# Four query blocks as two Strassen pairs ahead of the last gate pair

## The chip, the cores and the metric

The kernel runs on one core of a Trainium2 chip. The metric is device time in microseconds (us) of one execution. TensorE does the matrix products, VectorE (DVE in the profile) and ScalarE (ACT) the elementwise work, GpSimd (POOL) a few copies, and SyncE (SP) issues most of the DMA. Each engine has its own queue of instructions and works through it in order; an instruction waits at the head of its queue until the semaphores of what it needs have come. The order on each queue is fixed when the kernel is built: the code is written in some order, and a scheduler then arranges the instructions of each engine.

## The reference, cut to what matters

The layer mixes a prompt of 1024 tokens and 8 sample tokens (1032 columns, `TT`) by three branches that share one input projection, and merges them with gates.

```python
def mixer_block(xn, mem_k, mem_v, ...):
    sc_b, sc_c, sc_x, z, xbc, dt_raw, q, gates = jnp.split(xn @ w_in, splits, axis=-1)
    conv_u, sc_new = causal_depthwise_conv(sc_c * sc_x, sc_hist, sc_conv_w)
    y_a = (sc_b * conv_u) @ w_sc_out
    ...
    y_ssd, ssm_new = ssd_fn(xs, dt, a, bm, cm, ssm_s0)
    y_ssd = (y_ssd + ssm_d[:, None] * xs).reshape(bsz, seq, SSM_D_INNER) * jax.nn.silu(z)
    y_b = group_rmsnorm(y_ssd, ssm_norm_w, SSM_GROUPS) @ w_ssm_out
    qh = q.reshape(bsz, seq, ATTN_HEADS, ATTN_HEAD_DIM)
    scores = jnp.einsum('blhd,bmhd->bhlm', qh, mem_k).astype(jnp.float32) * (ATTN_HEAD_DIM ** -0.5)
    probs = jax.nn.softmax(scores, axis=-1).astype(mem_v.dtype)
    y_c = jnp.einsum('bhlm,bmhd->blhd', probs, mem_v).reshape(bsz, seq, ATTN_DIM) @ w_attn_o
    g_a, g_b, g_c = jnp.split(jax.nn.sigmoid(gates), N_BRANCHES, axis=-1)
    merged = g_a * y_a + g_b * y_b + g_c * y_c
    return merged @ w_merge_o, (sc_new, ssm_conv_new, ssm_new)
```

All is float32. `q` is 1024 columns of the projection, computed as eight blocks of 128 columns, 0 to 7. The change concerns how blocks 0 to 3 are computed, and what runs beside the scan (`ssd_fn`) after that.

## The kernel before, in words

**Products.** A float32 product is done as three products of a rounded high part and a low remainder (`hi*hi`, `hi*lo`, `lo*hi`). ScalarE casts the high part, VectorE subtracts it to get the low one, for weights (`weights`, lines 175 and 176) as for activations (`split_act`, lines 185 and 186). Activations lie transposed: 128 channels on partitions, 1032 tokens along the free side, 8 such tiles for 1024 channels.

There are two ways to do a block of 128 output columns:
- A *plain block* (`gemm3`, matmul in line 254): 8 input tiles, the columns in three thirds of 344, three products, so 72 matmuls of 128x344. `q_step`, `out_part` and others use it.
- A *Strassen pair* (`strassen`, with `st_prod`, matmul in line 306): two neighbouring blocks at once by 7 products of half size. Each product is 4 input tiles by three products by two halves of a 516-column half row (256 and 260 columns), so 168 matmuls for two blocks. The sums of the input halves (`xforms`) are made once for all pairs; the sums of the weight halves are made per pair by VectorE and ScalarE. `plain_pair` wraps it for the blocks of z and of the gates, applies the activation function and writes the two blocks to DRAM.

**The part of the program that matters here**, by the profiled execution:
- Projections in Strassen pairs, up to `gate_pair(22)`. Its hook `plain` fetches the weights of the first plain block, calls `load_group(0)` and remakes one set of the sums.
- The *scan stage*. 18 plain blocks run on TensorE: the eight query blocks wq0 to wq7, then the conv branch's output wo00 to wo07 (inputs: the eight tiles of `sc_d`), then wo10 and wo11 of the first half of the scan branch's output (inputs: tiles 0 to 7 of `yb_d`). In between, the pieces in the list `pend` are issued: for each of four groups (0 to 3) the scan's steps over eight chunks (`ssd_pieces`: small matmuls, then y and s updates, lines 1091 to 1149), the final state (`psf`, line 1165), four `z_pieces` (multiply by the silu of z and sum the squares into `sqa`, lines 1221 to 1232) and the group's norm (`group_norm`: three matmuls `psny`, line 1244, that average `sqa` over channels; then scaling, line 1267, and the stores to `yb_d`, line 1270).
- The *attention stage*: blocks wo12 to wo17, and wo20 to wo27 (second half of the scan branch, inputs: tiles 8 to 15 of `yb_d`), with the attention's pieces in between. Among them is the sample tokens' attention (`pso`, line 1726: one matmul group per sample over a freshly loaded megabyte of cached values, and `psob`, line 1743, which transposes the sample rows for the store to `at_d`).
- wo30 onwards: the attention branch's output, inputs `at_d`, and the rest of the layer.

**What sets the order.** `tick` issues the next piece of `pend`. A block that starts takes `pace[0]` pieces (with the fraction carried on in `pace[1]`) and spreads them evenly over its 24 steps (`marks`). Before the scan stage `pace` is set to the number of pieces divided by a number of blocks, so this number decides where in the sequence of blocks each piece falls. For the attention stage line 1845 sets it to the number of its pieces divided by the number of blocks left before wo30, less 1.4. When the first block of a new set of inputs starts (wo00, wo10, wo20, wo30), `out_in` loads and splits what `out_ahead` has not yet: `out_ahead`, called in the last block of the set before, loads two tiles and splits as the last third of that block goes along. A piece that is issued in the same stretch shares VectorE, ScalarE and SyncE's queue with these loads and splits. Weights of the next block are loaded one block ahead (`run_next`).

Of the kernel before, what the change touches and what calls it, by code (L numbers as in the profile page):

```python
# [11 lines left out]
AF = mybir.ActivationFunctionType  # L12
# [5 lines left out]
P = 128  # L18
D = 1024
T = 1024  # L20
NS = 8
TT = T + NS
# [4 lines left out]
KD = D // P  # L27
EPS = 1e-6
LAG = 3

QS = -1.0 / 16.0
GROUPS = 4
HEADS = 32
HPG = 8
# [5 lines left out]
C_SCB, C_SCC, C_SCX, C_Z, C_XBC, C_DT, C_Q, C_G = 0, 1024, 2048, 3072, 5120, 8192, 8224, 9248  # L40
# [3 lines left out]
def tile_kernel(ctx: ExitStack, tc, a, o):  # L44
    nc = tc.nc
    V, S, G, PE, SY = nc.vector, nc.scalar, nc.gpsimd, nc.tensor, nc.sync
# [95 lines left out]
    loaded = {}  # L142

    def load_raw(src, name):
        raw = wp.tile([P, 1024], F32, tag="raw", name=name + "r")
        if len(src.shape) == 3:
            in_turn("raw", SY.dma_start(raw.rearrange("p (k c) -> p k c", k=src.shape[1]), src))
        else:
            in_turn("raw", SY.dma_start(raw, src))
        return raw  # L150
# [28 lines left out]
    def ev_tile(name, shape=(P, TT + 4), dt=F32):  # L179
        return ev.tile(list(shape), dt, tag="ev", name=name)  # L180
# [8 lines left out]
    pend = deque()  # L189
# [12 lines left out]
    pace = [3, 0.0]  # L202
# [55 lines left out]
    def wblock(w, col):  # L258
        return w[:, col : col + P].rearrange("(k p) c -> p k c", p=P)
# [5 lines left out]
    HS = [slice(0, HT), slice(HT, TT)]  # L265
# [211 lines left out]
    q_d = dram("q_d", [8, P, TT])  # L477
# [10 lines left out]
    qs = cp.tile([P, 8, NS], F32, tag="qs", name="qs")  # L488

    w_in = a["w_in"][0]  # L490
# [456 lines left out]
        S.activation(t[:, :TT], flat(ps), AF.Silu)  # L947
        S.dma_start(zs_d[i], t[:, :TT])

    def plain_pair(col, dst, i, nm, func, hook=None, after_t3=None):  # L950

        os = []

        def outs():
            os.extend([pa_["u"](f"{nm}{i}"), pa_["u"](f"{nm}{i + 1}")])
            return os[0][:, HS[0]], os[0][:, HS[1]], None, os[1][:, HS[1]]

        pa = strassen(
            wblock(w_in, col + i * P), wblock(w_in, col + (i + 1) * P), xforms, f"{nm}{i}", pa_["s"], outs,
            hook=hook, after_t3=after_t3,  # L960
        )
        S.activation(os[0][:, :TT], os[0][:, :TT], func)
        S.dma_start(dst[i], os[0][:, :TT])
        S.activation(os[1][:, HS[1]], os[1][:, HS[1]], func)
        ins = S.activation(os[1][:, HS[0]], pa, func, scale=-1.0).ins
        S.dma_start(dst[i + 1], os[1][:, :TT])
        return ins

    def z_pair(i, hook=None):
        plain_pair(C_Z, zs_d, i, "Z", AF.Silu, hook)  # L970

    def gate_pair(i, after_t3=None):
        return plain_pair(C_G, gt_d, i, "G", AF.Sigmoid, None, after_t3)
# [495 lines left out]
    with_steps(3, lambda: gate_pair(18))  # L1469
    with_steps(2, lambda: gate_pair(20))  # L1470
    assert not steps
    rb = ev_tile("rb")
    SY.dma_start(rb[:, :TT], r_d.to_broadcast([P, TT]))
    b12s = []
# [14 lines left out]
            xg.append(t)  # L1489

    def plain():
        loaded["wq0"] = load_raw(wblock(w_in, C_Q), "wq0")
        load_group(0)
        for kt in range(4):
            split_to(*xforms["T3"][kt], b12s[kt // 2][:, HS[kt % 2]])
# [9 lines left out]
    for name in ("ssr", "ssd", "ssy"):  # L1505
        pool[name] = ssd.enter_context(tc.tile_pool(name=name, bufs=2, side="right"))
    fillers = deque()
    for i in range(8):
        fillers.extend(q_step(i))

    acts = []
# [67 lines left out]
    ins = ((sc_d, a["w_sc_out"][0]), (yb_d, a["w_ssm_out"][0, 0:D]), (yb_d[8:16], a["w_ssm_out"][0, D : 2 * D]), (at_d, None))  # L1579
# [15 lines left out]
    for g in range(GROUPS):  # L1595
# [8 lines left out]
        if g == GROUPS - 1:  # L1604
            norm[2] = lambda f=norm[2]: (f and f(), kv_ahead(0))
        pend.extend(z_pieces(g, xg, hold) + [None] + norm)
    pace[:] = len(pend) / (len(fillers) + KD + 2) + 1e-6, 0.0
    while fillers or pend:
        if len(fillers) == 1:
            out_ahead(sc_d)  # L1610
# [414 lines left out]
    for m in (0, 2):  # L2025
        nm = f"wm{m}"
        raw1, raw2, sa, wA, wS = begun if m == 0 else st_begin(wm[m], wm[m + 1], nm, ev_sums)
        residuals(m)
        pa, pb = (whole(mm_ps(nm + n)) for n in "ab")
# [34 lines left out]
    for m in last:  # L2064
        nm = f"wm{m}"
# [119 lines left out]
    for n, (j, j2) in enumerate(pairs):  # L2185
        s1, s2, pa = hidden_pair("g", j, j2)
# [3 lines left out]
        u1, u2, pa = hidden_pair("u", j, j2)  # L2190
# [34 lines left out]
    after_t3 = [None]  # L2225
# [258 lines left out]
```

## Time and profile before

| | |
|---|---|
| time, median of 3 runs | 2417.18 us (2413.96 to 2420.94) |
| the profiled execution's own time | 2418.97 us |
| its span (first to last instruction) | 2417.2 us |
| TensorE busy, 0 to 940 us | 930.14 |
| TensorE busy, 940 to 980 us (G20, G22) | 39.97 |
| TensorE busy, 980 to 1313 us (scan stage) | 329.58 of 333 |
| TensorE busy, 1313 to 1549 us (attention stage) | 230.61 of 236 |
| TensorE busy, 1549 to 2417 us (wo30 and the rest) | 858.04 of 868.2 |
| bytes moved, mean over the span | 167 GB/s |

The span is what the profiler saw between the first and the last instruction; 1.8 us of the profiled execution lie outside it. "PE" in a row is TensorE, "PEld" its weight loads. A row of the chain of waits has the start, the time on the chain, the engine, what ran (output, and input behind an arrow) and the line. A row of a timeline has the start, the duration, the engine, the line, the operation, the tiles and their shapes, and in square brackets the engine's idle time ahead of it and what ended it. A row of a table of windows has the stretch, its length, then for TensorE, its weight loads, VectorE, ScalarE and GpSimd the busy time and the number of instructions, then the granted TensorE clock, the share of DMA time and GB/s.

### The profile page before, as it was taken

The page shows a single profiled execution, that of the slowest core. Times are in us where ns is not written, and L with a number is a line of the kernel's source. Part 1 is how long each engine was busy: PE and PEld are TensorE (multiplying, and loading weights), DVE is VectorE, ACT ScalarE, POOL GpSimd, SP SyncE. Part 2 cuts the span into 40 slices and gives each one's busy share as a digit, 9 for nine tenths or more (in the row PEclk, how much of TensorE's full clock was granted, in tenths as well). Part 3 has the DMA queues.
Part 4 walks back from the last instruction along what each step waited for, and adds up shares of the span by engine and source line. Part 5 has one row for each costly group of instructions (what it writes and reads, how often), then busy time and mean ns, then how long its engine had stood idle before and what let it go on. Part 6 is the DMA issues. An engine that isn't in the chain of part 4 may idle for free.

```text
span 2417.2 us, 45099 instructions
## 1 busy us (share of the span) xinstructions
PE 2388.3 (99%) x18620; PEld 2305.3 (95%) x18620; DVE 1650.5 (68%) x2700; ACT 1101.1 (46%) x1794; POOL 129.3 (5%) x163
## 2 busy tenths in 40 slices
PE   8999999999999999999999999999999999999998
PEld 6999999999999999998998998899999999999998
DVE  6844677777777676568788664469687655567965
ACT  6643454555453543656656443214553333343423
POOL 0000000000000000223212000000000000000000
PEclk9999999999999999999999999999999999999999
DMA  6445423444354345768787787864346333354622
GB/s 201 140 149 166 132 88 115 134 147 128 109 158 119 101 140 167 234 214 279 257 286 238 234 321 242 276 215 145 118 159 175 103 96 105 93 182 151 194 90 78
DMA packets 348244, 403.74 MB, mean 167 GB/s; under 512 B 16014, under 2 KB 269054, under 8 KB 348031
## 3 DMA queue, kind: packets, MB, share of 16 engines
q1 hardware_dynamic: 324902, 337.60, 45.1%
q10 hardware_dynamic: 23137, 63.26, 6.8%
q8 instruction: 146, 2.39, 0.4%
q14 instruction: 59, 0.48, 0.1%
HBM read 284.65 MB, written 116.38 MB: 166 GB/s over the span
## 4 chain that ended last, share of the span: by engine, by line
PE 89%; DMA 4%; DVE 4%; ACT 1%; issue 1%; SPq 0%; ACTq 0%; DVEq 0%
PE po L254 8%; PE po L226 3%; PE ps_q L254 3%; PE pd L2295 1%; PE py L1130 1%; PE po L1121 1%; PE ps_z L226 1%; PE pss L1143 1%; PE G16m L306 1%; PE d00m L306 1%; PE G22m L306 1%; PE Z2m L306 1%; PE Z14m L306 1%; PE X4m L306 1%; PE Z12m L306 1%
## 5 line engine op out<-in xcount | busy, mean ns | idle before, releaser
L1073 ACT ACTIVATE r<-r,acum 128x128 f32<-128x128 f32 x256 | 79.3, 392 | 3.0 <-DMA r<-ac_d 2.4
L1106 POOL TENSOR_TENSOR xdd<-xdt,decst 128x512 f32<-128x512 f32 x32 | 51.1, 1596 | 248.3 <-DVE xdt L1102 246.1
L860 DVE SCALAR_TENSOR_TENSOR ax<-u,prm,ax 128x1024 f32<-128x1024 f32 x44 | 56.3, 1280 | 0.0
L1014 ACT ACTIVATE st<-st,es 128x128 f32<-128x128 f32 x128 | 41.4, 392 | 21.9 <-DMA st<-in_state_ssm_dram 19.1
L1564 DVE TENSOR_TENSOR yr<-po,yr 128x344 f32<-128x344 f32 x24 | 12.1, 514 | 45.9 <-PE po L254 32.5
L1100 DVE TENSOR_TENSOR r<-r,cbm 128x1024 f32<-128x1024 f32 x32 | 39.0, 1218 | 3.2 <-ACT r L1075 2.4
L1016 DVE SCALAR_TENSOR_TENSOR st<-sr,dts,st 128x128 f32<-128x128 f32 x128 | 40.3, 346 | 0.4
L1125 DVE TENSOR_TENSOR y<-po,ea 128x512 f32<-128x512 f32 x28 | 19.3, 689 | 25.4 <-PE po L1121 25.3
L1020 DVE SCALAR_TENSOR_TENSOR sr<-st,sr 128x128 f32<-128x128 f32 x128 | 35.3, 286 | 1.1
L1130 PE MATMUL py<-r,xdt 128*64 128x128 f32 x512 | 35.0, 279 | 0.7 <-DVE xdt L1102 0.7
L1676 DVE SCALAR_TENSOR_TENSOR kc<-kc,qb 128x256 f32<-128x256 f32 x64 | 24.2, 420 | 16.6 <-DMA qb<-qs_d 11.0
L1156 POOL TENSOR_TENSOR s<-s,cdec 128x512 f32<-128x512 f32 x28 | 34.8, 1244 | 4.1 <-DVE s L1149 3.5
L1143 PE MATMUL pss<-xdd,bT 128*128 128x512 f32 x64 | 33.0, 597 | 1.1 <-DVE y L1125 0.6
L1075 ACT ACTIVATE r<-r 128x1024 f32<-128x1024 f32 x32 | 33.8, 1056 | 0.6
L1130 PEld LDWEIGHTS py<-r,xdt 128*64 128x64 f32 x512 | 27.3, 136 | 5.0 <-DVE xdt L1102 1.4
L1121 PE MATMUL po<-bc,s 128*128 128x128 f32 x224 | 30.2, 278 | 0.8 <-DVE s L1149 0.8
L1121 PEld LDWEIGHTS po<-bc,s 128*128 128x128 f32 x224 | 28.0, 191 | 2.4 <-DVE s L1149 1.7
L1688 ACT ACTIVATE pr<-psa,mx 128x256 f32<-128x256 f32 x32 | 14.9, 473 | 29.7 <-DVE mx L1686 29.7
L863 DVE SCALAR_TENSOR_TENSOR ax<-u,prm,ax 128x1032 f32<-128x1032 f32 x22 | 28.3, 1287 | 0.0
L857 ACT ACTIVATE ax<-u,prm 128x1024 f32<-128x1024 f32 x22 | 27.4, 1246 | 1.2 <-ACT u L941 0.4
L1791 ACT CAST pTh<-psp 128x256 fp32r<-128x256 f32 x32 | 11.8, 374 | 32.9 <-DVE pTl L1792 24.0
L1102 DVE TENSOR_TENSOR xdt<-xp,dtT 128x512 f32<-128x512 f32 x32 | 22.0, 687 | 6.4 <-PE xp L1095 5.8
(8856 smaller groups left out, 9294.4 us busy)
## 6 DMA issues: line engine op xcount, KB each, us to landing
r<-ac_d SPq DMA_DIRECT2D x32, 512.0 KB
gt_d<-G ACTq DMA_DIRECT2D x24, 516.0 KB
gt<-gt_d SPq DMA_DIRECT2D x24, 516.0 KB
xs_d<-ax ACTq DMA_DIRECT2D x22, 516.0 KB
zs<-zs_d SPq DMA_DIRECT2D x16, 516.0 KB
yb_d<-x SPq DMA_DIRECT2D x16, 516.0 KB
in<-yb_d SPq DMA_DIRECT2D x16, 516.0 KB
st<-in_state_ssm_dram SPq DMA_DIRECT2D x32, 256.0 KB
```

The lines of the kernel that those rows point to most:

```text
L226: PE.matmul(po, wt[:, ks], xc, start=(k == 0 and i == 0), stop=(k == nk - 1 and i == 2))
L254: PE.matmul(pss[t][:, :CW], wt[:, ks], x[:, c], start=(k == 0 and i == 0), stop=(k == nk - 1 and i == 2))
L306: last_mm[0] = PE.matmul(po, wt[:, ks], xc, start=(start and kt == 0 and i == 0), stop=(kt == 3 and i == 2), skip_group_check=True,).ins
L860: V.scalar_tensor_tensor(acc[:, :T], u[:, j : j + T], w[j], acc[:, :T], op0=ALU.mult, op1=ALU.add)
L1014: S.activation(st[:, i], st[:, i], AF.Copy, scale=es[:, g * 4 + i, b : b + 1])
L1016: V.scalar_tensor_tensor(st[:, i], rb, dts[:, g * 4 + i, b : b + 1], st[:, i], op0=ALU.mult, op1=ALU.add)
L1073: S.activation(r[:, j, :], r[:, j, :], AF.Relu, scale=-1.0, bias=acum[:, c, h : h + 1])
L1100: V.tensor_tensor(r, r, bc(cbm.unsqueeze(1), [P, HPG, P]), op=ALU.mult)
L1106: G.tensor_tensor(b3(xdd, HPG), b3(xdt, HPG), bc(decst[:, c, hs].unsqueeze(2), [P, HPG, 64]), op=ALU.mult)
L1121: last = PE.matmul(po[:, t * P : (t + 1) * P], state["s"][:, t * P : (t + 1) * P], bcg[1][:, cs], start=True, stop=True,)
L1130: PE.matmul(py[hp : hp + 64, (h // 2) * P : (h // 2 + 1) * P], xdt[:, h * 64 : (h + 1) * 64], r[:, (h % 2) * 4 + h // 2, :], start=True, s ...
L1143: PE.matmul(pss, bT, xdd, start=True, stop=True)
```

## The change

Query blocks 0 to 3 are computed as two Strassen pairs, Q0 and Q2, between `gate_pair(20)` and `gate_pair(22)`. `plain_pair` gets a scale for them, and GpSimd copies the eight sample columns of each block to `qs`, which `q_step` does for a plain block. The plain blocks of the scan stage begin with wq4. The number that sets the pace is that of the fillers (now 4) plus 12 in place of plus 10: the scan's pieces are spread over 16 blocks, wq4 to wq7, wo00 to wo07 and wo10 to wo13, in place of 18. The attention stage gets 12 blocks, wo14 to wo27, in place of 14.

```diff
+QP = 4
...
-    def plain_pair(col, dst, i, nm, func, hook=None, after_t3=None):
+    def plain_pair(col, dst, i, nm, func, hook=None, after_t3=None, scale=1.0):
...
-        S.activation(os[0][:, :TT], os[0][:, :TT], func)
+        S.activation(os[0][:, :TT], os[0][:, :TT], func, scale=scale)
+        if dst is q_d:
+            G.tensor_copy(qs[:, i, :], os[0][:, T:TT])
         S.dma_start(dst[i], os[0][:, :TT])
-        S.activation(os[1][:, HS[1]], os[1][:, HS[1]], func)
-        ins = S.activation(os[1][:, HS[0]], pa, func, scale=-1.0).ins
+        S.activation(os[1][:, HS[1]], os[1][:, HS[1]], func, scale=scale)
+        if dst is q_d:
+            G.tensor_copy(qs[:, i + 1, :], os[1][:, T:TT])
+        ins = S.activation(os[1][:, HS[0]], pa, func, scale=-scale).ins
...
+    def q_pair(i):
+        plain_pair(C_Q, q_d, i, "Q", AF.Copy, scale=QS)
...
     with_steps(2, lambda: gate_pair(20))
     assert not steps
+    for i in range(0, QP, 2):
+        q_pair(i)
...
-        loaded["wq0"] = load_raw(wblock(w_in, C_Q), "wq0")
+        loaded[f"wq{QP}"] = load_raw(wblock(w_in, C_Q + QP * P), f"wq{QP}")
...
-    for i in range(8):
+    for i in range(QP, 8):
         fillers.extend(q_step(i))
...
-    pace[:] = len(pend) / (len(fillers) + KD + 2) + 1e-6, 0.0
+    pace[:] = len(pend) / (len(fillers) + KD + 4) + 1e-6, 0.0
```

**How the order moves.** In the rows below, a name ends in the scheduler's own number; po07 is the output of block wo07, b03 is the split input tile 3 of the running set (h high, l low), in03 its load. Lines of the kernel after stand 1 to 10 lower down than before.

The first place is the change of inputs from wo07 to wo10. In VectorE's queue of the kernel before, the subtractions of wo10's inputs stand among the scan steps of group 3 (y3, s3, r3, cbm3) and the gate products of wo07:

```order
L186 TENSOR_TENSOR b03l_14410<-in03_14345,b03h_14409 128x1032
L186 TENSOR_TENSOR b04l_14439<-in04_14376,b04h_14438 128x1032
L1125 TENSOR_TENSOR y3_14022<-po3_3_14265,ea3_3_14213 128x4x128
L1097 TENSOR_TENSOR cbm3_4_14307<-bp3_4_14299,tri_79 128x128
L1135 TENSOR_TENSOR y3_14022<-py3_3_14271,y3_14022 128x4x128
L1100 TENSOR_TENSOR r3_4_14141<-r3_4_14141,cbm3_4_14307 128x1024
L1102 TENSOR_TENSOR xdt3_4_14312<-xp3_4_14302,dtT_768 128x512
L1149 TENSOR_TENSOR s3_3_14244<-pss3_3_14324,s3_3_14244 128x512
L1560 TENSOR_TENSOR gt07_14200<-po07_0_14210,gt07_14200 128x344
L1560 TENSOR_TENSOR gt07_14200<-po07_1_14211,gt07_14200 128x344
L186 TENSOR_TENSOR b05l_14472<-in05_14413,b05h_14471 128x1032
```

In the kernel after, the same subtractions stand among the last pieces of group 2, x20 to x23 with the squares sqa2, behind the last chunk's y2 and s2:

```order
L1229 SCALAR_TENSOR_TENSOR x20_13383<-x20_13383,dpar_773,y2_13481 128x1032
L1157 TENSOR_TENSOR s2_7_14000<-pss2_7_14062,s2_7_14000 128x512
L1232 TENSOR_TENSOR x20_13383<-x20_13383,zs20_14011 128x1032
L1229 SCALAR_TENSOR_TENSOR x21_13386<-x21_13386,dpar_773,y2_13481 128x1032
L1229 SCALAR_TENSOR_TENSOR x22_13389<-x22_13389,dpar_773,y2_13481 128x1032
L1232 TENSOR_TENSOR x21_13386<-x21_13386,zs21_14013 128x1032
L1232 TENSOR_TENSOR x22_13389<-x22_13389,zs22_14091 128x1032
L1229 SCALAR_TENSOR_TENSOR x23_13392<-x23_13392,dpar_773,y2_13481 128x1032
L1240 TENSOR_TENSOR sqa2_14089<-sqa2_14089,zs21_14013 128x1032
L1232 TENSOR_TENSOR x23_13392<-x23_13392,zs23_14106 128x1032
L1240 TENSOR_TENSOR sqa2_14089<-sqa2_14089,zs22_14091 128x1032
L187 TENSOR_TENSOR b02l_14150<-in02_14115,b02h_14149 128x1032
```

On TensorE the means of that group (psny20 to psny22) now stand behind the tenth matmul of wo10:

```order
L255 MATMUL po10_0_14235<-b01h_14130,wo10l_14232 128x344
L255 MATMUL po10_0_14235<-b02h_14149,wo10h_14231 128x344
L255 MATMUL po10_0_14235<-b02l_14150,wo10h_14231 128x344
L255 MATMUL po10_0_14235<-b02h_14149,wo10l_14232 128x344
L255 MATMUL po10_0_14235<-b03h_14170,wo10h_14231 128x344
L1252 MATMUL psny20_14161<-sqa2_14089,ones_77 128x344
L1252 MATMUL psny21_14164<-sqa2_14089,ones_77 128x344
L1252 MATMUL psny22_14182<-sqa2_14089,ones_77 128x344
```

What moved is the end of group 2: it now falls in the block in which the inputs change. Before, the means of groups 0 to 3 stood in wq4 (behind 44 of its 72 matmuls), wo01 (27), wo05 (42) and wo11 (72); now they stand in wo00 (17), wo04 (46), wo10 (10) and wo14 (46).

The second place is the change of inputs from wq7 to wo00, where group 0 now ends. VectorE's queue of the kernel after has the subtractions b02l to b06l between the pieces of x02, x03 and sqa0 (line 1253 behind them reads the mean psny00):

```order
L1232 TENSOR_TENSOR x02_11586<-x02_11586,zs02_12396 128x1032
L187 TENSOR_TENSOR b02l_12442<-in02_12405,b02h_12441 128x1032
L1229 SCALAR_TENSOR_TENSOR x03_11588<-x03_11588,dpar_773,y0_11783 128x1032
L1240 TENSOR_TENSOR sqa0_12394<-sqa0_12394,zs02_12396 128x1032
L1232 TENSOR_TENSOR x03_11588<-x03_11588,zs03_12414 128x1032
L187 TENSOR_TENSOR b03l_12461<-in03_12426,b03h_12460 128x1032
L187 TENSOR_TENSOR b04l_12485<-in04_12445,b04h_12484 128x1032
L1240 TENSOR_TENSOR sqa0_12394<-sqa0_12394,zs03_12414 128x1032
L187 TENSOR_TENSOR b05l_12510<-in05_12464,b05h_12509 128x1032
L187 TENSOR_TENSOR b06l_12524<-in06_12488,b06h_12523 128x1032
L1253 TENSOR_SCALAR y0_11783<-psny00_12475 128x344
```

Before, group 0 ended in wq4, where no inputs are split, and these subtractions stood among the steps of the last two chunks of group 1 (py1_6 and py1_7), whose norm followed in wo01.

The third place is the end of the sample tokens' attention, ahead of wo30. On TensorE the transposes psob stand behind 4 of wo27's 72 matmuls in the kernel before:

```order
L254 MATMUL po27_0_17093<-b00h_15780,wo27h_17089 128x344
L254 MATMUL po27_0_17093<-b00l_15781,wo27h_17089 128x344
L254 MATMUL po27_0_17093<-b00h_15780,wo27l_17090 128x344
L254 MATMUL po27_1_17094<-b00h_15780,wo27h_17089 128x344
L1743 MATMUL psob_17025<-ident_72,osr_17023 128x8 x8
L254 MATMUL po27_1_17094<-b00l_15781,wo27h_17089 128x344
L254 MATMUL po27_1_17094<-b00h_15780,wo27l_17090 128x344
```

and behind 29 of them in the kernel after:

```order
L255 MATMUL po27_2_17171<-b02h_15791,wo27h_17165 128x344
L255 MATMUL po27_2_17171<-b02l_15792,wo27h_17165 128x344
L255 MATMUL po27_2_17171<-b02h_15791,wo27l_17166 128x344
L255 MATMUL po27_0_17169<-b03h_15819,wo27h_17165 128x344
L255 MATMUL po27_0_17169<-b03l_15820,wo27h_17165 128x344
L1753 MATMUL psob_17101<-ident_72,osr_17099 128x8 x8
L255 MATMUL po27_0_17169<-b03h_15819,wo27l_17166 128x344
L255 MATMUL po27_1_17170<-b03h_15819,wo27h_17165 128x344
```

So 68 matmuls of wo27 stood between psob and the first matmul of wo30, and now 43 do.

## The prediction

> **What bounds the kernel now.** I read the page's span, busy shares and chain first.
>
> ```profile
> span 2417.2 us, 45099 instructions
> PE 2388.3 (99%) x18620; PEld 2305.3 (95%) x18620; DVE 1650.5 (68%) x2700; ACT 1101.1 (46%) x1794; POOL 129.3 (5%) x163
> PE 89%; DMA 4%; DVE 4%; ACT 1%; issue 1%; SPq 0%; ACTq 0%; DVEq 0%
> ```
>
> TensorE is busy in 2388.3 of 2417.2 us: time goes down if it gets less work, and up if it pauses. So I looked next at how the two stages that change are filled, and how close the others come to holding TensorE up (table of windows: stretch, length, then TensorE, weight loads, VectorE, ScalarE, GpSimd, clock, DMA share, GB/s).
>
> ```profile
> 940.00:960.00 20.00, 20.00 (x170) 20.00 (x170) 11.23 (x15) 7.80 (x11) 0.00 (x0) 1.00 0.35 111
> 980.00:1313.00 333.00, 329.58 (x2357) 299.07 (x2356) 256.07 (x318) 198.74 (x417) 94.71 (x68) 1.00 0.77 250
> 1130.00:1160.00 30.00, 29.49 (x191) 27.89 (x191) 28.45 (x32) 17.26 (x24) 1.90 (x2) 1.00 0.91 311
> 1313.00:1549.00 236.00, 230.61 (x1539) 215.78 (x1538) 125.64 (x306) 90.21 (x192) 0.00 (x0) 0.99 0.78 263
> ```
>
> Over the scan stage TensorE idles 3.4 us in 333. But in 1130 to 1160, where group 1 of the scan ends, VectorE is busy 28.45 of 30 us: there it is as full as TensorE, and anything added to it in such a stretch must show.
>
> **What is removed.** Four plain blocks become two Strassen pairs. The chain of waits (start, us on the chain, engine, tile, line, count) gives both pitches.
>
> ```profile
> 940.10 20.02 PE G20m L306 x168
> 1051.17 12.14 PE ps_q L254 x77
> ```
>
> A pair is 168 matmuls in 20.02 us; a plain matmul takes 12.14/77 = 157.7 ns, so a block of 72 takes 11.35 us and four take 45.4. Two pairs take 40.04. **Saving: 5.4 us.** The work that comes with a pair (weight sums, splits, scaling) lies under its matmuls: beside G20 VectorE had 11.23 and ScalarE 7.80 of 20 us to do, DMA .35. I cost it at nothing, and the GpSimd copies of 8 columns too, since GpSimd is idle there. Without that cover a pair would cost at most VectorE's 11.23 us, which no row suggests.
>
> **What moves.** The same scan pieces stand over 16 blocks. VectorE's timeline shows what the end of a group asks of it (group 1, before).
>
> ```profile
> 1133.70 0.68 DVE L1135 TENSOR_TENSOR y<-py,y 128x512 f32<-128x512 f32 x1
> 1134.30 1.22 DVE L186 TENSOR_TENSOR b06l<-in,b06h 128x1032 fp32r<-128x1032 f32 x1
> 1135.44 0.68 DVE L1149 TENSOR_TENSOR s<-pss,s 128x512 f32<-128x512 f32 x1
> 1136.04 2.48 DVE L1221 SCALAR_TENSOR_TENSOR x<-x,dpar,y 128x1032 f32<-128x1032 f32 x2
> 1138.44 2.37 DVE L1224 TENSOR_TENSOR x<-x,zs 128x1032 f32<-128x1032 f32 x2
> 1140.73 1.22 DVE L186 TENSOR_TENSOR b07l<-in,b07h 128x1032 fp32r<-128x1032 f32 x1
> ...
> 1148.88 1.35 DVE L1560 TENSOR_TENSOR gt<-po,gt 128x344 f32<-128x344 f32 x3
> 1150.15 1.23 DVE L1232 TENSOR_TENSOR sqa<-sqa,zs 128x1032 f32<-128x1032 f32 x1
> ```
>
> ```profile
> 1136.17 0.66 PE L1165 MATMUL psf<-ident,s 128*128 128x128 f32 x4 [0.51 <-DVE s L1149]
> 1151.64 1.90 PE L1244 MATMUL psny<-sqa,ones 128*128 128x344 f32 x6
> ```
>
> From the last y at 1133.70 to the end of the last sum of squares at 1151.38 VectorE runs back to back for 17.68 us, and TensorE's means (psny) start 0.26 us behind it. By the starts of neighbouring rows a pitch is 0.6 us for y and s, 1.2 for a piece's first multiply, 1.15 for its second, for a sum and for a subtraction of inputs, and 1.27 for the three gate products.
>
> *wo00.* Group 0 now ends where the inputs change. Without b06l, b07l and the gate products of that row, but with five subtractions (b00l to b04l) in front of psny00, the chain is 17.68 - 1.14 - 1.15 - 1.27 + 5 x 1.15 = 19.9 us. TensorE has in front of psny00 the last 72 matmuls of wq7 and 17 of wo00: 89 x 0.1577 = 14.0 us, with psf 0.66 and the state product:
>
> ```profile
> 1254.81 1.12 PE pss L1143 x2
> ```
>
> 1.1 us, together 15.8. **Pause: 4.1 us**, in one place or spread over the waits for b02 to b04. Bounds: 2, if two subtractions get done in gaps ahead of the last y; 7, if in02's load, which stands in SyncE's queue behind the store of group 0's final state, comes late too.
>
> *wo10.* Group 2 ends here. Up to b02l VectorE has 0.6 + 0.6 + 4 x 1.2 + 4 x 1.15 + 2 x 1.15 + 1.15 = 14.05 us; TensorE has 32 matmuls of wo07 and 7 of wo10, 6.15 us, and 1.8 of scan products, 7.9 in all. That is a pause of 6.1, and the last sum (1.15 us against three matmuls) adds 0.7 in front of psny20. **6.8 us**; bounds 4 (y two matmuls earlier and b02l taken between pieces) and 8. Before, wo10's subtractions had a whole block of time, from the first to the last of these rows, and no piece of a group's end among them:
>
> ```profile
> 1250.74 1.23 DVE L186 TENSOR_TENSOR b00l<-in,b00h 128x1032 fp32r<-128x1032 f32 x1 [0.42 <-ACT b00h L185]
> ...
> 1284.42 1.40 DVE L186 TENSOR_TENSOR b07l<-in,b07h 128x1032 fp32r<-128x1032 f32 x1
> ```
>
> *wo20.* The chain has a stall here that the change may remove.
>
> ```profile
> 1410.73 7.13 DMA in<-yb_d
> 1419.39 4.12 PE po L254 x15
> ```
>
> ```profile
> PE po L254 <- ACT yr L1562: 3.1, 1, 3.1
> ```
>
> ```profile
> 1420.00:1425.00 5.00, 5.00 (x29) 5.00 (x28) 3.90 (x5) 3.96 (x6) 0.00 (x0) 0.73 0.82 258
> ```
>
> TensorE waits 3.07 us (the row rounds it to 3.1) for the first inputs; behind that the clock is 0.73 and 15 matmuls take 4.12 us instead of 2.37, 1.75 more. The inputs come late because SyncE has them behind a load of cached keys:
>
> ```profile
> 1408.16 0.33 SPq L1669 DMA_DIRECT2D kc<-in_cache_mem_k_dram  x1
> 1408.59 10.69 SPq L1517 DMA_DIRECT2D in<-yb_d  x6
> ```
>
> In the order after, four of the six stand ahead of that load. Group 3 ends a block later relative to wo20, so its stores are later too. **Gain 3 us**, between 0 and 4.8.
>
> *The sample attention's end.* These are serial steps that the pace now gives 12 blocks instead of 14.
>
> ```profile
> 1536.95 0.66 PE L1743 MATMUL psob<-ident,osr 8*128 8x8 f32 x8
> 1548.64 0.94 PE L254 MATMUL po<-b00h,wo30h 128*128 128x344 f32 x3
> ```
>
> ```profile
> 1538.59 3.24 DMA at_d<-o_s
> 1542.87 6.10 DMA in<-at_d
> ```
>
> From psob to wo30 the store, the load, the cast and the subtraction take 11.7 us; before, 68 matmuls lay over them (10.7 and psob's 0.66) and TensorE hardly waited. Now 43 do, 6.8 + 0.66 = 7.4. **Pause 4.3 us**; bounds 0 (psob itself early) and 5.5. In front of it each sample's value product waits for a megabyte that is fetched once the last one is copied out:
>
> ```profile
> 1502.07 1.07 PE L1726 MATMUL pso<-vc,pTs 128*32 128x256 f32 x16
> 1509.81 0.64 PE L1726 MATMUL pso<-vc,pTs 128*32 128x256 f32 x8 [0.25 <-DMA vc<-in_cache_mem_v_dram]
> ```
>
> ```profile
> 1503.21 6.56 DMA vc<-in_cache_mem_v_dram
> ```
>
> The fetch of 6.56 us just fits. After, 24 matmuls and a product (4.9 us) and 27 (5.3) stand in two of these gaps: 1.7 + 1.3 less what an earlier wait shifts, **2 us**, between 0 and 4.
>
> *The clock.* After the 3.07 us pause it cost 1.75. Three new pauses are longer than that; I take two of them to cost as much, since wo00's may come in parts: **3.5**, between 0 and 5.2. [...]
>
> **Sum:** -5.4 + 4.1 + 6.8 - 3 + 4.3 + 2 + 3.5 = +12.3 us. The profiled execution took 2418.97 us, 1.8 more than its span and as much more than the median of the runs, 2417.18; so I expect 2431.3 of a profiled execution like that one, and 2429.5 of the median.
>
> **The rivals.**
>
> *The pauses don't come* (faster). One mechanism decides: VectorE and ScalarE take the splits of wo00 and wo10 before the group's end, in the gaps that 256.07 busy of 333 us leave, so the means are not late and psob isn't either. What stays is -5.4 and wo20's stall going whole, -4.8: 2407. It holds if the three pauses together are under 3 us. For it: before, VectorE worked off b06l and b07l inside a group's end and TensorE idled only 0.51 us in 1130 to 1160. Against it: the queues are in order, and in the order after the subtractions stand between the pieces.
>
> *The pauses come at half size* (same): 2.1 + 3.4 + 2.2 + 1 + 1.75 - 3 - 5.4 = +2, 2419. For it: my lags are counted to the matmul, and a late y is worked off where TensorE waits for it anyway.
>
> *The attention stage becomes bound by transfers* (slower than forecast). It moved 263 GB/s x 236 us = 62 MB at a share of .78; in two blocks less, 236 - 2 x 11.35 = 213 us, less their weights and inputs, 60 MB need 282 GB/s. If no more than 263 passes, it takes 228 us, 15 more: 2445. Against it: 1130 to 1160 shows 311 GB/s at .91.
>
> **How the numbers follow.** The forecast has 0.58, with 2422 to 2441 as its own range; half-sized pauses 0.18, no pauses 0.14, bound by transfers 0.10. The range from 2412 to 2441 leaves out most of the no-pause case and of the transfer case. A measurement here tells about 0.3%, 7.25 us, from no change. Faster than 2409.9: 0.11, the no-pause case less a part. Slower than 2424.4: 0.55 of the forecast, the transfer case and a little of the halves, 0.66. Between: 0.23.
>
> **What would show it.** The matmuls of Q0 and Q2 take 20 us a pair, and VectorE and ScalarE keep up. TensorE's waits list psny in wo00 and wo10 behind sqa, or the first products there behind b02l to b04l, with 4 and 7 us. No 3 us wait stands at wo20's first matmul, and one of about 4 at wo30's, with the clock under 1 behind it. Wrong would be: TensorE idle no longer than 10 us between the first query pair and wo30 (no pauses), or idle in many small waits for cached keys and values (transfers), or pairs longer than 20 us.

## The result and the profile after

The kernel after takes 2436.99 us (median of 4 runs, 2434.2 to 2437.77) against 2417.23 us: a ratio of 1.0079 with a 95% interval of 1.0062 to 1.0097, so it is slower, by 19.8 us. 2429.5 was predicted, in a range of 2412 to 2441. The profiled execution took 2437.18 us, its span is 2435.5.

The page of the kernel after:

```profile
span 2435.5 us, 45201 instructions
PE 2388.8 (98%) x18668; PEld 2303.6 (95%) x18668; DVE 1659.9 (68%) x2718; ACT 1106.8 (45%) x1798; POOL 119.1 (5%) x163
```

TensorE's busy time is 2388.8 us as against 2388.3, though it has less to do, and the span grew by 18.3: what was added is idle time, and a slower TensorE. Where it waits stands in the table of waits of the kernel after (engine, line, what released it: us in total, times, longest):

```profile
PE po L255 <- DVE b02l L187: 5.8, 2, 5.4
PE po L255 <- DVE b03l L187: 3.9, 1, 3.9
PE po L255 <- ACT b00h L186: 3.1, 1, 3.1
PE psa L1780 <- ACT q00h L186: 2.9, 1, 2.9
PE psv L1812 <- ACT pTh L1801: 1.9, 2, 1.3
PE po L255 <- ACT q L911: 1.3, 1, 1.3
...
PE po L255 <- ACT b02h L186: 1.0, 1, 1.0
PE pso L1736 <- DMA vc<-in_cache_mem_v_dram: 0.5, 1, 0.5
```

The two longest are the two changes of inputs: b02l in wo10 and b03l in wo00. b00h in front of wo30 is the third. The 3.1 at wo20 is gone from the table. All that the change can touch lies between G20 and the first matmul of wo30, but for the slow clock behind the pause there. The table of windows has that stretch in one row, before:

```profile
939.94:1548.64 608.70, 599.86 (x4227) 554.37 (x4225) 401.31 (x649) 308.32 (x641) 94.71 (x68) 1.00 0.76 250
```

and after:

```profile
939.54:1564.18 624.64, 601.31 (x4274) 552.04 (x4272) 413.88 (x670) 315.07 (x645) 84.82 (x68) 0.98 0.74 245
```

It is 15.9 us longer: 14.5 of them TensorE's idle time (8.8 before, 23.3 after), 1.4 its busy time. The other 2.4 us of the span lie in stages whose code is the same. 1.7 of them are matmul time that the half clock behind the pause at wo30 costs (estimated further down). What is left is less than those stages differ by from run to run (the stretch up to G20 took between 938.0 and 942.3 us), so I count it as scatter.

**The pairs cost what was reckoned.** The chain of waits of the kernel after:

```profile
959.72 20.02 PE Q0m L307 x168
979.74 20.02 PE Q2m L307 x168
```

They take 40.04 us without a gap. So 5.4 us of matmul time are saved, and yet the busy time of the stretch is up by 1.4: TensorE's other work took 6.8 us more. By the record of the granted clock, TensorE was busy for 15.0 us at half speed in this stretch (5.50, 6.09 and 3.41), and for 3.33 before. Taking half of that as lost, an estimate, gives 7.5 us and 1.7, which is 5.8 of the 6.8; the last 1.0 stays open. The windows of the kernel after around three of the pauses show the slow clock (the column behind the five engines):

```profile
1099.80:1103.70 3.90, 0.03 (x1) 0.00 (x0) 3.90 (x5) 2.96 (x4) 0.00 (x0) 1.00 0.44 146
1103.70:1107.00 3.30, 1.95 (x5) 1.51 (x6) 2.19 (x2) 3.22 (x6) 0.02 (x1) 0.51 0.34 101
1107.00:1110.30 3.30, 3.30 (x8) 2.28 (x8) 3.04 (x5) 2.00 (x2) 0.20 (x1) 0.50 0.81 259
...
1262.90:1268.30 5.40, 0.00 (x0) 0.00 (x0) 5.40 (x6) 4.28 (x5) 0.00 (x0) 0.62 0.10 42
1268.30:1271.00 2.70, 2.68 (x6) 1.80 (x7) 2.70 (x3) 0.00 (x0) 0.00 (x0) 0.50 0.59 176
1271.00:1274.20 3.20, 3.20 (x9) 2.25 (x8) 2.47 (x5) 2.42 (x3) 0.00 (x0) 0.50 0.79 228
...
1564.10:1567.40 3.30, 3.22 (x12) 3.12 (x13) 3.15 (x3) 2.67 (x4) 0.00 (x0) 0.57 0.78 218
```

In both pauses VectorE is busy all the time (3.90 of 3.90, 5.40 of 5.40) while TensorE does nothing; behind them the clock stays at half for some 6 us. In wo10 it falls within the pause already (0.62 in that row).

**VectorE's queue at wo10**, timeline of the kernel after:

```profile
1254.02 0.69 DVE L1143 TENSOR_TENSOR y<-py,y 128x512 f32<-128x512 f32 x1 [0.30 <-PE py L1138]
1254.75 1.29 DVE L1229 SCALAR_TENSOR_TENSOR x<-x,dpar,y 128x1032 f32<-128x1032 f32 x1
...
1260.11 2.37 DVE L1232 TENSOR_TENSOR x<-x,zs 128x1032 f32<-128x1032 f32 x2
...
1265.89 1.23 DVE L1240 TENSOR_TENSOR sqa<-sqa,zs 128x1032 f32<-128x1032 f32 x1
1267.03 1.23 DVE L187 TENSOR_TENSOR b02l<-in,b02h 128x1032 fp32r<-128x1032 f32 x1
```

From the last y at 1254.02 to the end of b02l at 1268.26 there are 14.2 us with no idle time noted in any row (14.05 was reckoned), and TensorE's matmul on b02l starts at 1268.31.

### The profile page after: what moved, and what is told of

The parts are those of the page before. It is cut to its first block, busy times and chain, and to the rows that moved or that the text cites. A ratio compares the mean times of both kernels' runs of the same rounds, so it can differ in the third digit from the quotient of the medians.

```text
span 2435.5 us, 45201 instructions
## 1 busy us (share of the span) xinstructions
PE 2388.8 (98%) x18668; PEld 2303.6 (95%) x18668; DVE 1659.9 (68%) x2718; ACT 1106.8 (45%) x1798; POOL 119.1 (5%) x163
## 4 chain that ended last, share of the span: by engine, by line
PE 87%; DMA 5%; DVE 5%; ACT 2%; issue 1%; SPq 0%; ACTq 0%; DVEq 0%
PE po L255 8%; PE po L227 3%; PE py L1138 1%; PE ps_q L255 1%; PE pd L2305 1%; PE pss L1151 1%; PE po L1129 1%; PE ps_z L227 1%; PE G16m L307 1%; PE Z2m L307 1%; PE d10m L307 1%; PE Z14m L307 1%; PE X18m L307 1%; PE Z6m L307 1%; PE Z10m L307 1%
## 5 line engine op out<-in xcount | busy, mean ns | idle before, releaser
L1574 DVE TENSOR_TENSOR yr<-po,yr 128x344 f32<-128x344 f32 x24 | 11.9, 512 | 39.5 <-PE po L255 33.9
L1107 ACT COPY bT<-bp 128x128 f32<-128x128 f32 x32 | 8.4, 263 | 61.1 <-DVE cbm L1105 61.1
```

## The experiments

All were run beside the kernel before on the same chip. "Stretch" is the time from G20 to wo30 in the profile, as in the two rows above, "idle" TensorE's idle time in it.

| | median us | ratio to before (95%) | stretch | idle |
|---|---|---|---|---|
| before | 2417.23 | | 608.7 | 8.8 |
| after | 2436.99 | 1.0079 (1.0062 to 1.0097) | 624.6 | 23.3 |
| 1: no pairs, 16 blocks | 2432.65 | 1.0068 (1.0056 to 1.0081) | 623.4 | 20.3 |
| 2: pairs, 18 blocks | 2432.45 | 1.0059 (1.0044 to 1.0073) | 621.2 | 22.5 |
| 3: one pair, 16 blocks | 2422.2 | 1.0018 (1.0009 to 1.0027) | 611.9 | 12.5 |
| 4: after, with idle matmuls | 2447.95 | 1.0125 (1.0109 to 1.0142) | 634.7 | 26.3 |
| 5: after, less VectorE work in group 2 | 2429.78 | 1.0049 (1.0034 to 1.0064) | 621.7 | 22.4 |
| 6: after, 1.7 in the attention's pace | 2427.32 | 1.0045 (1.0028 to 1.0062) | 617.4 | 17.7 |
| 7: pairs, 14 blocks | 2433.03 | 1.0063 (1.0048 to 1.0078) | 621.9 | 18.5 |
| 8: one pair, 17 blocks | 2422.16 | 1.0020 (1.0011 to 1.0030) | 612.4 | 13.1 |
| 9: after, scan 8 pieces later | 2439.18 | 1.0095 (1.0082 to 1.0108) | 629.3 | 28.4 |
| 10: pairs, 17 blocks, 2.0 | 2435.15 | 1.0075 (1.0059 to 1.0091) | 624.5 | 22.9 |
| 11: one pair, 18 blocks, 1.7 | 2424.26 | 1.0034 (1.0022 to 1.0046) | 615.0 | 15.6 |
| 12: before, loads by ScalarE | 2417.94 | 1.0002 (0.9993 to 1.0011) | 611.6 | 9.8 |

### 1. The pace without the pairs

```diff
 (in the kernel before)
-    pace[:] = len(pend) / (len(fillers) + KD + 2) + 1e-6, 0.0
+    pace[:] = len(pend) / (len(fillers) + KD) + 1e-6, 0.0
```

> The kernel before with its scan pieces over 16 blocks instead of 18, and no Strassen pairs for the query blocks. In its order groups 1 and 3 of the scan end in wo00 and wo10, as groups 0 and 2 do in the kernel after. Theory (a group's end and the new inputs share VectorE's queue, and TensorE is slowed behind the pause): pauses of 3 to 6 us at wo00 and at wo10, each with 2 to 4 us of half clock behind it, no pause at wo30, and no saving of 5.4: some 10 to 16 us slower than before, 2427 to 2433, with no pair in it at all. Rival (the pairs themselves or the attention stage's 12 blocks cost the time): within 3 us of before, no pause over 2 us at wo00 or wo10.

2432.65 us, 15.1 over the kernel before in the same runs. Timeline of TensorE:

```profile
1140.80 0.66 PE L254 MATMUL po<-b02l,wo00h 128*128 128x344 f32 x1 [4.43 <-DVE b02l L186]
...
1305.32 0.66 PE L254 MATMUL po<-b02l,wo10h 128*128 128x344 f32 x1 [6.08 <-DVE b02l L186]
```

The two pauses of the kernel after stand here with no query block in a Strassen pair, and there is no wait over 0.5 us at wo30's first matmul. This is the theory's case, and the rival falls: the pairs don't make these pauses. What this kernel shares with the kernel after is that two groups end where the inputs change.

### 2. The pairs without the pace

```diff
-    pace[:] = len(pend) / (len(fillers) + KD + 4) + 1e-6, 0.0
+    pace[:] = len(pend) / (len(fillers) + KD + 6) + 1e-6, 0.0
```

> The kernel after with its scan pieces over 18 blocks, as before, so that the attention stage gets 10 blocks. In its order the groups end in wo01, wo05, wo11 and wo16, in no block in which the inputs change. Theory: no pause over 2 us at wo00 and wo10; psob comes 22 plain matmuls later in front of wo30 than in the kernel before the change plus 18 more than after it, so a pause of about 7 us at wo30 with 2 to 4 us of half clock, and shorter waits for cached values: 2417 - 5.4 - 4.8 + 7 + 3 + 2 to 6 = 2419 to 2423. Rival (pairs cost the time by themselves): 2437 or more, with waits in or right behind Q0 and Q2, or pauses at wo00 and wo10 as in the kernel after.

There is no wait over 0.5 us at wo00 and at wo10, and the one at wo30 came as forecast. But the time is 10 us over the forecast. From this kernel's table of waits:

```profile
PE po L255 <- ACT b00h L186: 6.2, 1, 6.2
PE psv L1813 <- DVE pTl L1802: 2.8, 1, 2.8
...
PE pss_sc L1712 <- DVE kc L1686: 2.3, 2, 1.2
```

The first row is wo30. The others are many: in wo20 to wo30 TensorE idles 15.3 us, 9 of them not at wo30. The attention's work doesn't fit under 10 blocks. So the blocks that the pairs take out are missed later, which neither side of this test had priced: the rival's waits at the pairs, at wo00 and at wo10 are not there either.

### 3, 8 and 11. One pair only

```diff
 (3)
-QP = 4
+QP = 2
-    pace[:] = len(pend) / (len(fillers) + KD + 4) + 1e-6, 0.0
+    pace[:] = len(pend) / (len(fillers) + KD + 2) + 1e-6, 0.0
 (8: QP = 2, and KD + 3)
 (11: QP = 2, KD + 4 as in the kernel after, and 1.7 for 1.4 in the attention's pace)
```

> One pair (query blocks 0 and 1) and the scan's pieces over 16 blocks (six query blocks, wo00 to wo07, wo10, wo11): as many blocks as in the kernel after, 14 for attention as before. In its order the groups end in wq6, wo02, wo06 and wo12, in no block in which the inputs change. Theory: no pause over 2 us at wo00, wo10 and wo30; saving 2.7 of the pair, 0 to 5 at wo20: 2410 to 2416. Rival (16 blocks are too few for the scan's work, wherever its groups end): pauses of several us in the blocks with a group's end, over 2422.

> One pair and the scan's pieces over 17 blocks. In its order the groups end in wq6, wo02, wo07 (behind 4 of its matmuls) and wo13 (behind 3), psob stands at the end of wo26, 4 matmuls earlier than before the change. Theory: no pause over 2 us at wo00, wo10, wo20 and wo30; saving 2.7, and up to 4.8 where wo20's wait was: 2411 to 2417. Rival (fewer blocks cost by waits for the groups' transfers, as with one pair and 16 blocks): 2419 to 2424.

> One pair, the scan's pieces over 18 blocks as before, 12 for attention, and 1.7 instead of 1.4 in the pace of the attention stage. In its order the groups end in wq6, wo03, wo07 (behind 37) and wo13, psob stands behind 1 matmul of wo27. Theory (all three costs are avoided, and the scan is as thin as before): no pause over 2 us from the pair to wo30, saving 2.7 of the pair and up to 4.8 at wo20: 2410 to 2417, the first that is under the kernel before. Rival (the attention stage in 12 blocks costs what the pair saves): 2418 to 2423, with new waits of 1 to 3 us in it.

All three are misses of the theory's numbers: 2422.2, 2422.16 and 2424.26 us, slower than before by 0.2 to 0.3%. By their times numbers 3 and 8 lie in their rivals' ranges, number 3 at the very edge, and number 11 lies above its own. The places come out as in their orders: at wo00, the first two wait no more than 1.1 us and the third 1.6; at wo30 none waits over 1.1. But 12.5 to 15.6 us of idle time (8.8 before) are spread over many waits. Row of the table of waits of number 3:

```profile
PE xp L1103 <- DMA x<-xs_d: 4.7, 3, 2.1
```

These are the first products of a group, which wait for the group's tiles from DRAM (before, this wait is not among the 20 longest). In number 11 wo10 waits again:

```profile
1271.63 0.79 PE L255 MATMUL po<-b03h,wo10h 128*128 128x344 f32 x3 [3.17 <-ACT b03h L186]
```

So with one pair most of the loss of the kernel after is gone, but its saving of 2.7 us stands against 3.7 to 6.8 us more of idle time. These runs don't separate what takes the loss away, since one pair also leaves two plain blocks more as cover. With both pairs, numbers 2, 7 and 10 keep the groups' ends out of wo00 and wo10 too, and are still 15 to 20 us over the kernel before.

### 4. Idle matmuls in the pauses

```diff
+DUMMY = {("po00", 3, 1): 24, ("po10", 2, 1): 34}
...
+                if t == 0 and (name, k, i) in DUMMY:
+                    pd = sm_ps(f"dum{name}")
+                    prev["pe"] = mm_.ins
+                    for _ in range(DUMMY[name, k, i]):
+                        in_turn("pe", PE.matmul(pd[:, :CW], hi[:, :P], acts[0][0][:, c], start=True, stop=True))
```

> The kernel after with 58 matmuls that nobody reads, 128x344 each, 24 in front of the first that takes b03l in wo00 and 34 in front of the first that takes b02l in wo10, that is in the places where TensorE waits 3.9 and 5.4 us: 9.1 us of work more. Theory of the clock (the half clock behind a pause comes from TensorE having been idle and costs about 3 us at each place): no half clock at wo00 and wo10, 4 to 6 us faster than the kernel after, 2431 to 2433, though it does more. Rival (the slow stretch has another cause, such as the transfers or the scan's matmuls behind it): the half clock stays and the time is that of the kernel after or up to 9 us more, 2437 to 2446.

2447.95 us, 11 over the kernel after and over both forecasts. The timeline shows why it tells nothing of the clock:

```profile
1271.37 3.78 PE L1260 MATMUL psny<-sqa,ones 128*128 128x344 f32 x6 [6.87 <-DVE sqa L1248]
...
1277.47 5.52 PE L260 MATMUL dumpo<-b00h,wo10h 128*128 128x344 f32 x34
```

The scheduler put the means, and with them the wait, in front of the added matmuls, so these ran behind the pause and not in it; at wo00 they ran behind the pause as well. The question whether work in the pause would keep the clock up stays open by this run.

### 5. Less work for VectorE at the end of group 2

```diff
-            V.tensor_mul(xg[t], xg[t], zs)
+            n = 8 if g == 2 else TT
+            V.tensor_mul(xg[t][:, :n], xg[t][:, :n], zs[:, :n])
```

> The kernel after, with the product of group 2 with the silu of z cut from 1032 columns to 8 (four instructions of VectorE, 1.15 us each, in front of wo10's third input; the rest of the columns stays unmultiplied, so the outputs that hang on group 2 differ). Nothing else on VectorE, ScalarE or the queues of transfers is taken away. Theory (VectorE's work in a row sets the pause at wo10): from the last y to b02l it has 8 to 10 us to do instead of 14.2, against 7.9 of TensorE, so the 6.4 us of waits for b02 shrink to 0.5 to 2.5, no half clock in wo10, and the whole is 6 to 9 us under the kernel after, 2428 to 2431. The pause at wo00 stays at 4 to 5.5. Rival (the inputs of wo10 come late from DRAM, or ScalarE's casts are late): 5 us or more of waits for b02 stay, time within 3 us of the kernel after.

2429.78 us, within the forecast. The waits for b02 are gone, the one at wo00, which was left alone, is the same to 0.01 us, and there is one at wo15 that the kernel after doesn't have:

```profile
1102.15 0.66 PE L255 MATMUL po<-b03l,wo00h 128*128 128x344 f32 x1 [3.90 <-DVE b03l L187]
...
1260.36 0.42 PE L255 MATMUL po<-b00h,wo10h 128*128 128x344 f32 x1 [0.75 <-DVE gt L1571]
...
1362.54 0.66 PE L255 MATMUL po<-b00h,wo15h 128*128 128x344 f32 x1 [3.93 <-ACT yr L1573]
```

The clock is back too (the window over the same stretch of wo10 has 0.70 in the kernel after):

```profile
1258.00:1275.00 17.00, 15.39 (x89) 13.80 (x88) 15.47 (x20) 14.89 (x15) 0.00 (x0) 1.00 0.77 254
```

Only VectorE's work was taken, the inputs come from DRAM and through ScalarE's casts as before: this shows that VectorE's queue sets the pause at wo10, and that the half clock goes when the pause goes. The gain in the stretch from wo10 to wo20 is 4.8 us (157.0 as against 161.8), since it has the 3.9 us of wait at wo15. That the time fell within the forecast is in part luck: the whole stretch from G20 to wo30 is only 3.0 us shorter (621.7, 624.6), because wo20 to wo30 took 2.2 us longer, and the rest of the gain lies in stages of the same code.

### 6. An earlier end of the sample tokens' attention

```diff
-        pace[:] = len(pend) / (len(outs) - 1.4) + 1e-6, 0.0
+        pace[:] = len(pend) / (len(outs) - 1.7) + 1e-6, 0.0
```

> The kernel after with 1.7 in place of 1.4 in the pace of the attention stage, which puts psob behind 1 of wo27's matmuls instead of 29. Theory (the pause in front of wo30 is the serial way from psob to wo30 less the matmuls that lie over it): no pause over 1 us at wo30, the waits at wo00 and wo10 as in the kernel after, 3 to 5 us under it: 2432 to 2434. Rival (the attention's pieces are held up by transfers, so that an earlier place only moves the wait): waits for cached values or for psv grow by as much, time within 2 us of the kernel after.

2427.32 us, 9.7 under the kernel after, where 3 to 5 were forecast. No wait is left from wo20 to wo30 that is over 0.5 us, and psob has 11.9 us to wo30 (10.7 in the kernel after, of which 3.1 were a pause):

```profile
1543.71 0.66 PE L1753 MATMUL psob<-ident,osr 8*128 8x8 f32 x8
1555.57 0.32 PE L255 MATMUL po<-b00h,wo30h 128*128 128x344 f32 x1
```

The stretch from wo20 to wo30 is 6.5 us shorter (135.6 as against 142.1). The forecast had only the 3.1 us of pause; the 1.9 us of waits for psv are gone as well, and with the pause the half clock that stood behind it (1.00 from 1555 to 1560, the loss in wo30 was estimated at 1.7 us). The rest of the difference in time is within the scatter of the other stages. Set beside number 1 it also gives the price of the pairs roughly: both have the pauses at wo00 and wo10 and none at wo30's first matmul, though they differ in smaller waits, and with the pairs the stretch is 6.0 us shorter (617.4, 623.4), where 5.4 were reckoned.

### 7 and 10. Both pairs with 14 and 17 blocks

```diff
 (7)
-    pace[:] = len(pend) / (len(fillers) + KD + 4) + 1e-6, 0.0
+    pace[:] = len(pend) / (len(fillers) + KD + 2) + 1e-6, 0.0
 (10: KD + 5, and 2.0 for 1.4 in the attention's pace)
```

> Both pairs and the scan's pieces over 14 blocks (wq4 to wo11), so that the attention stage keeps its 14 as before. In its order the groups end in wq7, wo03, wo07 and wo12, psob stands behind 4 of wo27's matmuls as before. Theory (it matters where the groups end): at most 2 us of waits at wo10, some at wo00 since group 0 ends just in front of it (0 to 5), none over 1 us at wo30: 2412 to 2422. Rival (16 blocks, and all the more 14, are too few for the scan's work on VectorE wherever it lies): pauses of 2 us and more at every group's end, 2425 to 2440.

> Both pairs, the scan's pieces over 17 blocks, and 2.0 instead of 1.4 in the pace of the attention stage. In its order the groups end in wo01, wo05, wo11 and wo16, and psob stands behind 1 matmul of wo27. Theory: no wait over 1.5 us at wo00, wo10 and wo30; what is left against the saving of 5.4 is the attention stage in 11 blocks, 3 to 8 us of waits (10 blocks had 15 with 6 of them at wo30): 2415 to 2422. Rival (the attention stage cannot be shortened by three blocks): 8 to 15 us of waits in it, 2423 to 2432.

In both the theory's time is missed; with 14 blocks the rival's is met, with 17 blocks the time is 3 us above the rival's as well. With 14 blocks (2433.03 us) the means stand clear of wo10, but VectorE is late all the same, in the last block ahead of it and within it. Rows of its timeline:

```profile
1251.94 0.43 PE L255 MATMUL po<-b00h,wo07h 128*128 128x344 f32 x1 [3.13 <-DVE gt L1570]
...
1273.75 2.07 PE L1129 MATMUL po<-bc,s 128*128 128x128 f32 x8 [3.62 <-DVE s L1154]
```

With 17 blocks (2435.15 us, and a wide scatter, 2425.25 to 2439.23) no wait over 1.3 us is left at wo00, wo10 and wo30, as the theory had it, but of its 22.9 us of idle time most lie elsewhere. Rows of its table of waits:

```profile
PE psp L1794 <- DVE pr L1704: 5.6, 5, 2.8
PE po L255 <- ACT yr L1572: 3.9, 1, 3.9
PE xp L1103 <- DMA x<-xs_d: 3.6, 3, 2.7
```

### 9. The scan half a block later

```diff
+    pend.extend([None] * 8)
     for g in range(GROUPS):
         xg, bcg, hold = groups[g]
```

> The kernel after with eight empty pieces in front of the scan's, so that the scan starts some half block later over the same 16 blocks. In its order group 0 ends in wo01 and the last y of group 0 comes behind the subtraction b04l of wo00, instead of in front of all of them; at wo10 group 2's pieces now stand between b02l and b03l, with some 40 matmuls of wo10 and wo11 done. Theory (VectorE's pieces of a group's end, if they stand between the subtractions of a change of inputs, make the pause): no wait over 1.5 us at wo00 and no half clock there, 7 to 9 us less between wo00 and wo10 than in the kernel after; at wo10 a pause of 6 to 11 us, now for b03. Together 2428 to 2436. Rival (with 16 blocks the pauses come whatever the place): 3 us or more of waits between wo00 and wo02 all the same, at the place of the group's end.

2439.18 us, 3 over the upper end, with the waits at both places as forecast: nothing over 0.5 us at wo00 and no half clock there (1.00 from 1095.66 to 1242.60), and at wo10, where the pieces now stand between the subtractions, two waits for b03 in place of one for b02:

```profile
1265.87 0.94 PE L255 MATMUL po<-b03h,wo10h 128*128 128x344 f32 x2 [4.76 <-ACT b03h L186]
1272.06 0.66 PE L255 MATMUL po<-b03l,wo10h 128*128 128x344 f32 x1 [4.68 <-DVE b03l L187]
```

They are 9.4 us together, within the 6 to 11; the clock is at half for 13.7 us there, 6.7 of them idle. From wo00 to wo10 it is 16.0 us shorter than the kernel after (146.9, 162.9), where 7 to 9 were forecast, and from wo10 to wo20 20.7 longer (182.5, 161.8), as the pieces fall later. The same pieces over the same 16 blocks make a pause or none, by what they fall on.

### 12. The kernel before, with wo20's loads from another queue

```diff
-        SY.dma_start(t[:, :TT], src[k])
+        (S if src is yb2 else SY).dma_start(t[:, :TT], src[k])
```

> The kernel before, with the eight loads of wo20's inputs issued from ScalarE's queue instead of SyncE's, so that they don't stand behind a load of cached keys that waits 6 us for its buffer. Nothing of the change is in it. Account of the wait at wo20 in the prediction (3.07 us of wait and 1.75 of slow clock, from that load in SyncE's queue): no wait over 1 us at wo20's first matmul, no half clock there, 3 to 5 us under the kernel before, 2412 to 2415. Rival (the six loads are late for another reason, such as their own tiles or the stores of group 3): the wait stays at 2 us or more, or ScalarE stands still behind a load and TensorE waits for it elsewhere; 2416 to 2421.

2417.94 us, a ratio of 1.0002 (0.9993 to 1.0011): no gain, the rival's case. ScalarE's timeline (issues by its queue are ACTq):

```profile
1403.42 0.33 ACTq L1517 DMA_DIRECT2D in<-yb_d  x1
...
1412.28 1.06 ACT L185 CAST b02h<-in 128x1032 fp32r<-128x1032 f32 x1 [6.39 <-DMA in<-yb_d]
1412.34 0.33 ACTq L1517 DMA_DIRECT2D in<-yb_d  x1
```

In the kernel before, its casts and copies were:

```profile
1415.32 1.06 ACT L185 CAST b02h<-in 128x1032 fp32r<-128x1032 f32 x1 [8.74 <-DMA in<-yb_d]
...
1418.90 0.44 ACT L1562 COPY yr<-po 128x344 f32<-128x344 f32 x1
```

The load for b02 leaves 5 us earlier than in the kernel before (1403.42, against 1408.59), but is cast only 3 us earlier; the one for b04 leaves behind that cast. TensorE waits 2.5 us in wo20, for b03, instead of 3.07, and the stretch is not shorter. The place in SyncE's queue, which the prediction named, is not the whole cause of the wait at wo20; how much the transfers beside it take was not tried. The last two rows also set a reading of the prediction right: TensorE did not stand still for the first inputs there, but for a PSUM tile of wo17 (L1562), whose copy stood in ScalarE's queue behind the casts of b02 to b04, and so behind the late load.

## Why the prediction was right, point by point

It forecast a time 12.3 us up, by pauses where group ends meet changes of inputs. 19.8 were measured.

| term | forecast | measured |
|---|---|---|
| pairs for plain blocks | -5.4 | -5.3 (40.1 us more from G20 to the first plain matmul, less 45.4) |
| pause at wo00 | 4.1 | 4.2 for b02l and b03l, and 1.3 for a PSUM tile that ScalarE empties late |
| pause at wo10 | 6.8 | 6.4 (1.0 for b02h, 5.4 for b02l) |
| wo20 | -3 | -4.7 (3.07 of wait and 1.7 of clock, an estimate, both gone) |
| pause at wo30 | 4.3 | 3.1 |
| cached values (pso) | 2 | 0.3 |
| clock | 3.5 | 9.2, an estimate (1.7 of it in wo30, behind the end of the stretch) |
| start of attention, psv | none | 1.6 and 1.9 |

These terms come to 18.0, and to 16.3 without the 1.7 that lies behind the end of the stretch. The stretch grew by 15.9. The parts agree less well than their sum: the waits in the table come to 15.7 us where the idle time grew by 14.5, and the terms of matmul time to 0.6 where the busy time grew by 1.4.

- **The mechanism was right, and is shown.** Number 1 makes the pauses without the pairs, number 9 moves them by moving the pieces, number 5 takes one away by taking VectorE's work alone. The two chains of the prediction came out at 14.2 us for 14.05 at wo10; at wo00 VectorE was back to back too, from the last y at 1085.80 to the end of b03l at 1103.67, and the whole chain to the last sum of squares, reckoned at 19.9, took 21.4 us, 1.1 of them a wait for ScalarE.
- **What was mis-sized is the clock.** "I take two of them to cost as much", 1.75 each, is the term that came out too small, by 5.7 us and beyond its own bound of 5.2. By the record of the granted clock, half speed lasted 6.83 us at wo00 (1.33 of them idle), 10.24 at wo10 (4.15 idle), and 3.41 each behind q00h and in wo30. Half of the matmul time in them, an estimate by that clock, is 2.8, 3.0, 1.7 and 1.7 us. By the starts of neighbouring plain matmuls, 0.287 us apart at half speed (1419.85 to 1422.43 in the kernel before, nine of them) and 0.158 at full, 45% would be lost, 0.9 us less in all. So four pauses had a price, not two, and two of them a higher one than the pause of the kernel before from which it was taken. Behind the two of 2.93 and 3.06 us the clock was 0.56 (1369.60 to 1373.00) and 0.57 (1564.10 to 1567.40), so pauses no longer than the one before had their price as well. Why two of the stretches are longer was not shown.
- **wo20** was right in sign and a little small, within its bounds; its reason was only partly so, by number 12.
- **psob to wo30** took 10.7 us instead of the 11.7 of before, under the reckoned 7.4 of cover: 3.1. Number 6 shows that this pause goes when the pace alone is changed.
- **Not forecast:** the wait for q00h where attention begins, 2.93 where 1.36 stood before, and 1.9 for psv. Both lie in the attention stage, where TensorE idled 5.4 us before (14 blocks), 8.7 after (12), 12.5 in number 10 (11) and 18.7 in number 2 (10). Number 6 idles only 3.6 in the same 12 blocks, with the wait for q00h and without those for psv. So with 12 blocks it is the pace that costs; with 10 and 11 one pace each was tried.
- **The rivals.** That the pauses come at half size, or not at all, is out by the rows. The attention stage bound by transfers is out in its form (275 GB/s went through after, from wo14 to wo30, and 263 before), but the shortage of blocks in it, which stood behind that rival, shows with 10 blocks: 15.3 us of idle time from wo20 to wo30.

No version with pairs that was run is faster than the kernel before: the two pairs save 5.4 us, and in every order tried the four plain blocks that they take away had been cover for more than that.

## What to carry to other kernels

Where independent blocks of matmuls serve as cover for other work, a cheaper block is also less cover: price the change by what stands under the cover at its end, not by the matmul time saved. When a pacing number moves, list what each burst of work on the second engine now falls on, and count that engine's queue from its last input to the first product that waits; this gave both pauses within 0.5 us here, not counting the wait for a PSUM tile at wo00. And price the slower clock behind every pause, not only behind the longest: in the kernel after, pauses of 2.9 to 5.4 us were followed by a loss estimated at 1.7 to 3.0 us each.

## What the runs showed of the hardware

From G20 to wo30 the record of the granted clock of the kernel after has half speed from 1103.74, 1264.17, 1369.98 and 1564.54 us, for 6.83, 10.24, 3.41 and 3.41 us; the kernel before has it once, from 1419.31 for 3.41 us. The pauses with which they go are of 3.89, 5.43, 2.93 and 3.06 us after, and of 3.07 before.

The length of a pause alone doesn't decide whether half speed follows. One of 3.05 us in number 4 (psv, from 1436.35) is followed by full speed; TensorE idles 1.4 and 1.6 us in the first two of these windows:

```profile
1434.37:1437.79 3.42, 1.99 (x10) 1.37 (x8) 3.42 (x16) 1.43 (x2) 0.00 (x0) 1.00 1.02 373
1437.79:1441.20 3.41, 1.80 (x11) 1.75 (x12) 3.18 (x6) 2.10 (x4) 0.00 (x0) 1.00 1.02 420
1441.20:1444.61 3.41, 3.41 (x17) 2.87 (x16) 1.29 (x2) 0.09 (x1) 0.00 (x0) 1.00 0.95 323
```

One of 2.04 us in number 8 (in wo10) is followed by half speed; TensorE idles 2.1 and 0.4 us in the first two of these windows:

```profile
1266.27:1269.68 3.41, 1.33 (x7) 0.75 (x5) 3.41 (x5) 3.10 (x9) 1.38 (x1) 1.00 1.03 324
1269.68:1273.09 3.41, 3.04 (x18) 2.85 (x20) 2.45 (x6) 3.38 (x5) 1.52 (x2) 0.50 0.96 349
1273.09:1276.50 3.41, 3.41 (x28) 2.76 (x24) 3.41 (x4) 0.15 (x1) 0.00 (x0) 1.00 0.93 344
```

Nor is a long pause always there. In the kernel before, ahead of G20 in a stage that the change doesn't touch, TensorE idles 0.7 us in 3.41, and half speed follows:

```profile
43.73:47.14 3.41, 2.74 (x16) 1.75 (x15) 2.85 (x6) 1.68 (x5) 0.00 (x0) 1.00 0.17 46
47.15:50.56 3.41, 3.41 (x14) 2.83 (x14) 1.27 (x3) 1.54 (x5) 0.00 (x0) 0.50 0.79 227
```

This is read from the traces after the fact; what decides it was not shown, and no run was made to test it.
